# State-space layer of a decoder trunk: the convolution of x moved from channels on partitions to tokens on partitions

## The chip, the cores and the metric

The kernel runs on one core of one Trainium2 chip. The metric is device time in microseconds, the median of several executions. A core has five engines with queues of their own: PE (TensorE: matmuls; the loads of its stationary operand are shown apart as PEld), DVE (VectorE), ACT (ScalarE), POOL (GpSimd) and SP (SyncE), which only issues DMAs here. ACT and POOL issue some DMAs too.

## The reference, cut to what matters

The trunk is one latent-attention (MLA) layer and one state-space (SSM, Mamba-2) layer over 256 tokens, each followed by a dense squared-ReLU MLP; D_MODEL is 2048, the SSM's inner width 4096 (8 groups of 512 channels, 8 heads of 64 each) and everything is float32. What the change touches is this:

```python
def causal_depthwise_conv(x, w, b):            # width 4, each channel by itself
    C = x.shape[-1]
    out = lax.conv_general_dilated(
        x, w[:, None, :], window_strides=(1,), padding=[(SSM_CONV_WIDTH - 1, 0)],
        dimension_numbers=('NWC', 'WIO', 'NWC'), feature_group_count=C)
    return out + b

def ssm_mixer(h, w_in, conv_w, conv_b, ...):
    zxbcdt = h @ w_in
    z, xbc, dt = jnp.split(zxbcdt, [SSM_D_INNER, SSM_D_INNER + SSM_CONV_DIM], axis=-1)
    xbc = jax.nn.silu(causal_depthwise_conv(xbc, conv_w, conv_b))
    xs, b_in, c_in = jnp.split(xbc, [...], axis=-1)
    ...
    y = ssd_chunked_scan(xs, dt, a, b_in, c_in)    # one chunk of 256 tokens here
    y = y + d_skip * xs
    y = y * jax.nn.silu(z); y = group_rms_norm(y) * norm_g
    return y @ w_out
```

For each token and channel of x, B and C the projection is summed with the three tokens before it, by four weights, a bias is added, and silu is applied.

## The kernel before

Every matmul with a large weight goes over blocks of 512 output columns and both halves of 128 tokens (t = 0, 1). A weight is read in units of 128 x 1024 float32 (512 KB) by SP into one of six `raw` buffers (L87). ACT makes its rounded part `wh` (L102), DVE the rest `wl` (L103), four buffers of each, and PE runs 8 matmuls with wh (L325, L326) and 4 with wl (L329). `Flow.next` loads six units ahead and converts three ahead of the unit that PE is at. A block of the SSM is four pieces of two units, and after each piece `tick()` runs what was put off with `later(n, fn)`: fn runs n + 1 ticks on. The order on PE is the written one. The order on the other engines is arranged when the program is built, by when operands are expected to be ready; the written order breaks ties.

The SSM stage runs B0, dt, B1, C0, C1 and then the list `SSM_ORDER`: x blocks (projection of one group of 512 x channels), z blocks (the gate) and o blocks (output projection).

- `conv` (L1063) takes a block of x, B or C that lies with tokens on partitions (`ev`, evacuated by L1093). In each of two halves it turns 2 x 128 channels onto partitions with four PE transposes (L1070), multiplies by the last weight and adds the bias on ACT (L1076), adds the other three shifted products on DVE (L1079: weight a scalar per partition, shift along the free axis), and makes silu from tanh (L1081, L1082).
- B and C are used in that layout (`cb_group`, L1153). x is needed with tokens on partitions, so `x_block`'s `back` (L1173) turns it back, four transposes for each t (L1179), and evacuates it (L1181) into `xtm`.
- Then the eight heads of the group are put on the list `hq`; `pump`, run once a tick, takes one or two: SP reads a row of `cumD` (running sums of the decay, kept in DRAM) to all partitions (`cm`, L1215), ACT and DVE make the decayed score matrix `mt` (L1219 to L1222), and after eight heads `products` runs the matmuls with x (L1237), and POOL and DVE add the skip term (L1240 to L1243). `across` (L1193) adds the part of the first 128 tokens to the second.
- `z_block` (L1250) computes the gate; its `gate`, two ticks later, multiplies on POOL (L1268), norms, and transposes the result for the o blocks (L310).

In the two MLPs, POOL issues 56 DMAs that add a weight quarter to a buffer on arrival (L199).

Of the kernel before, what the change touches and what calls it, by code (L numbers as in the profile page):

```python
# [28 lines left out]
P = 128  # L29
# [185 lines left out]
class Trunk:  # L215
# [822 lines left out]
    def ssm_body(self, sp, dp, gain):  # L1038
# [21 lines left out]

        self.later(0, setup)

        def conv(ev, ct, dst, lag, after):  # L1063

            def half(j):
                b = self.bank(early[0])
                for k in range(2):
                    for t in range(2):
                        o = k * 256 + t * P
                        nc.tensor.transpose(b[:, o:o + P], ev[t][:, (2 * j + k) * P:(2 * j + k + 1) * P], self.ident)  # L1070
                a = self.scratch()
                for k in range(2):
                    c = ct + 2 * j + k
                    wc = lambda i: cst[:, C_CW + 4 * c + i:C_CW + 4 * c + i + 1]
                    s, o = b[:, k * 256:(k + 1) * 256], a[:, k * 256:(k + 1) * 256]
                    nc.scalar.activation(o, s, AF.Identity, bias=cst[:, C_CB + c:C_CB + c + 1], scale=wc(3))  # L1076
                    for i in (2, 1, 0):
                        m = 3 - i
                        nc.vector.scalar_tensor_tensor(o[:, m:256], s[:, 0:256 - m], wc(i), o[:, m:256], ALU.mult, ALU.add)  # L1079
                th = self.scratch()  # L1080
                nc.scalar.activation(th, a, AF.Tanh, scale=0.5)  # L1081
                nc.vector.scalar_tensor_tensor(dst(j), th, 1.0, a, ALU.add, ALU.mult)  # L1082
            self.later(lag, lambda: half(0))
            self.later(lag + 1, lambda: half(1))
            if after:
                self.later(4, lambda: after(0))
                self.later(5, lambda: after(1))

        def evac(accs):
            ev = []  # L1090
# [6 lines left out]
        def bc_block(name, i):  # L1097
            accs = self.block([("si", name, i, q) for q in range(4)], xT)
            t = self.ktile(self.k4, F32)
            fm[name, i] = t  # L1100
            conv(evac(accs), (32 if name == "B" else 40) + 4 * i,
                 lambda j: t[:, 2 * j:2 * j + 2].rearrange("p a b -> p (a b)"), 0, None)

        def dt_block():
            self.narrow_block(("si", "dt", 0, 0), self.xT, dt_chain)
# [1 line left out]
        def dt_chain(b):  # L1107
            pairs = [sp.tile([P, S], F32, tag="cm", name=f"dt{i}", bufs=4).rearrange("p (i t h) -> p i t h", i=2, t=2) for i in range(3)]
            v, e, s, z, q, la = (pairs[i // 2][:, i % 2] for i in range(6))
            for t in range(2):  # L1110
                nc.vector.scalar_tensor_tensor(v[:, t], b[:, t * 64:(t + 1) * 64], rs[t], cst[:, C_DTB:C_DTB + 64],
                                               ALU.mult, ALU.add)
            nc.scalar.activation(e, v, AF.Abs)
            nc.scalar.activation(e, e, AF.Exp, scale=-1.0)
            nc.vector.tensor_scalar(s, e, 2.0, None, ALU.add)
            nc.vector.reciprocal(s, s)
            nc.vector.tensor_tensor(s, s, e, ALU.mult)
            nc.vector.tensor_tensor(z, s, s, ALU.mult)
            nc.vector.tensor_scalar(q, z, 1.0 / 17, None, ALU.mult)
            for c in (15, 13, 11, 9, 7, 5, 3):  # L1120
                nc.vector.scalar_tensor_tensor(q, q, 1.0 / c, z, ALU.add, ALU.mult)
            nc.vector.scalar_tensor_tensor(q, q, 1.0, s, ALU.add, ALU.mult)
            nc.vector.tensor_scalar(v, v, 0.0, None, ALU.max)
            nc.vector.scalar_tensor_tensor(dt, q, 2.0, v, ALU.mult, ALU.add)
            for t in range(2):
                nc.vector.scalar_tensor_tensor(la[:, t], dt[:, t], -1.0, aneg, ALU.mult, ALU.mult)
            cum = sp.tile([64, S], F32, name="cum")

            def cums():
                b = self.bank(False)  # L1130
                nc.tensor.matmul(b[:64, 0:256], la[:, 0], tri, start=True, stop=False)
                nc.tensor.matmul(b[:64, P:256], la[:, 1], tri[:, 0:P], start=False, stop=True)
                nc.scalar.activation(cum, b[:64, 0:256], AF.Copy)
                nc.scalar.dma_start(cumD, cum)
                self.later(0, back)

            def back():
                b = self.bank(False)
                for t in range(2):
                    nc.tensor.transpose(b[:, t * 64:(t + 1) * 64], cum[:, t * P:(t + 1) * P], self.ident[:64, :64])  # L1140
                nc.tensor.matmul(b[:, 128:192], tri[:, P:256], la[:, 0], start=True, stop=True)
                nc.vector.tensor_copy(pcum.rearrange("p t h -> p (t h)"), b[:, 0:128])

                for t in range(2):
                    nc.vector.tensor_tensor(edge[:, t], b[:, 128:192], pcum[:, t], ALU.subtract)
                nc.scalar.activation(edge[:, 0], edge[:, 0], AF.Exp)
                nc.scalar.activation(edge[:, 1], edge[:, 1], AF.Exp, scale=-1.0)
                nc.vector.tensor_tensor(edge[:, 0], edge[:, 0], dt[:, 0], ALU.mult)
                nc.vector.tensor_scalar(edge[:, 1], edge[:, 1], 2.0, None, ALU.mult)

            self.later(2, cums)

        def cb_group(g):  # L1153
# [1 line left out]
            b = self.bank(early[0])  # L1155
            nc.tensor.matmul(b[:, 0:256], B[:, 0:P], C, start=True, stop=True)
            nc.tensor.matmul(b[:, 256:384], B[:, P:256], C[:, P:256], start=True, stop=True)
            t = sp.tile([P, 384], F32, name=f"cb{g}")
            for o in (0, 256):
                nc.vector.scalar_tensor_tensor(t[:, o:o + P], b[:, o:o + P], 0.125, tri[:, 0:P], ALU.mult, ALU.mult)  # L1160
            nc.scalar.activation(t[:, P:256], b[:, P:256], AF.Copy, scale=0.125)
            cb[g] = t

        def x_block(g):
            accs = self.block([("si", "x", g, q) for q in range(4)], xT)
            ev = evac(accs)
            fmx = [None, None]

            def dst(j):
                fmx[j] = self.scratch()  # L1170
                return fmx[j]

            def back(t):  # L1173
                if t == 0:
                    xg[g] = []
                b = self.bank(False)
                for k in range(4):
                    o = (k % 2) * 256 + t * P
                    nc.tensor.transpose(b[:, k * P:(k + 1) * P], fmx[k // 2][:, o:o + P], self.ident)  # L1179
                x = sp.tile([P, 512], F32, tag="xtm", name=f"xtm{g}_{t}", bufs=6)  # L1180
                nc.scalar.activation(x, b, AF.Copy)  # L1181
                xg[g].append(x)
                if t == 0:
                    return
# [6 lines left out]
                nc.gpsimd.tensor_tensor(heads_of(xw), heads_of(xg[g][0]), spread(edge[:, 0]), ALU.mult)  # L1191

                def across():  # L1193
                    b = self.bank(False)
# [16 lines left out]
        def head(g, i, dg):  # L1211
# [1 line left out]
            h = 8 * g + i  # L1213
            cm = sp.tile([P, S], F32, tag="cm", name=f"cm{h}", bufs=4)
            nc.sync.dma_start(cm, cumD[h:h + 1].to_broadcast([P, S]))  # L1215
            m = sp.tile([P, 256], F32, tag="mt", name=f"mt{h}", bufs=11)
            half = lambda t: m[:, t * P:(t + 1) * P]
            for t in range(2):
                nc.scalar.activation(half(t), cm[:, t * P:(t + 1) * P], AF.Relu, bias=pcum[:, t, h:h + 1], scale=-1.0)  # L1219
# [61 lines left out]
            assert 2 * i in gated and 2 * i + 1 in gated  # L1281
            return self.block([("so", 2 * i + q, nb) for q in range(2)], self.from_tiles(yT[2 * i:2 * i + 2]))

        bc_block("B", 0)
        dt_block()
        bc_block("B", 1)
        bc_block("C", 0)
        bc_block("C", 1)
        for g in range(GROUPS):
            self.later(2 + g % 2 + 4 * (g // 2), lambda g=g: cb_group(g))  # L1290
        self.pump = pump
        for step in SSM_ORDER:
            kind, i = step[0], int(step[1])
            if step == "x2":
                early[0] = False
            if kind == "x":
                x_block(i)
            elif kind == "z":
                z_block(i)
# [3 lines left out]
            else:  # L1303
# [81 lines left out]
def sequence(d):  # L1385
# [40 lines left out]
    si("B", 0)  # L1426
    add(("si", "dt", 0, 0), d["sidt"], 16, 64)
    si("B", 1), si("C", 0), si("C", 1)
    so = lambda k, nb: add(("so", k, nb), d["so"][k, nb])
    for step in SSM_ORDER:  # L1430
        kind, i = step[0], int(step[1])
        if kind in "xz":
            si(kind, i)
        elif i < 3:
# [85 lines left out]
```

## Time and profile before

| | |
|---|---|
| median of 3 runs | 2308.83 us (2308.43 to 2308.88) |
| span of the profiled execution | 2306.1 us; its own time is not given apart from the span |
| SSM stage in it | 952 to 1619 us |
| granted PE clock | 1.000 |
| busy: PE, DVE, ACT, POOL | 2298.4, 1890.2, 1419.4, 187.9 us |
| DMA | 510.77 MB, mean 221 GB/s |

The span runs from the first to the last instruction. Matmuls are pipelined, so a busy PE is not a PE at its peak; the cost of a PE instruction is read from the starts of its neighbours. In rows of groups the two numbers after the bar are busy time in us and mean ns of one, then idle time of the engine before them and what ended it.

### The profile page before, as it was taken

To read this page: it belongs to the slowest core of one execution; us is meant where nothing else is said; L and a number is where in the kernel's file an instruction comes from. 1 tells how busy PE (TensorE), PEld (TensorE's weight loads), DVE (VectorE), ACT (ScalarE), POOL (GpSimd) and SP (SyncE) were. 2 spreads that over 40 slices of the span, in tenths; PEclk is the share of its full clock that TensorE was granted. 3 is DMA by queue.
4 is the path that set the end of the run, shared out by engine and by line. 5 is a ranking of instruction groups with operands and counts; after the bars stand their busy time and mean duration, and the time that the engine had idled before them with its cause. 6 is when DMAs were issued, how large, how long until landed. Compare 5 with 4: busy or idle time off the path is not lost.

```text
span 2306.1 us, 30756 instructions
## 1 busy us (share of the span) xinstructions
PE 2298.4 (100%) x11057; PEld 1911.1 (83%) x11057; DVE 1890.2 (82%) x2318; ACT 1419.4 (62%) x1995; POOL 187.9 (8%) x227
## 2 busy tenths in 40 slices
PE   9999999999999999999999999999999999999999
PEld 7888888888888888888888888888888888888887
DVE  7786697999899897678788767756989989989895
ACT  7775466566666656575577555545666656666663
POOL 1430000000000000000022001110000000000000
PEclk9999999999999999999999999999999999999999
DMA  8444677877887877665566656556687788787874
GB/s 316 148 129 155 200 233 245 262 239 250 265 243 247 267 217 241 198 211 180 169 204 207 223 181 204 186 191 201 201 257 234 250 265 250 241 268 240 250 230 161
DMA packets 152153, 510.77 MB, mean 221 GB/s; under 512 B 17152, under 2 KB 26304, under 8 KB 152000
## 3 DMA queue, kind: packets, MB, share of 16 engines
q1 hardware_dynamic: 143712, 479.37, 62.7%
q0 software_dynamic: 8064, 29.36, 7.6%
q8 instruction: 87, 1.43, 0.3%
q14 instruction: 66, 0.54, 0.1%
q10 hardware_dynamic: 224, 0.07, 0.0%
HBM read 506.58 MB, written 2.16 MB: 221 GB/s over the span
## 4 chain that ended last, share of the span: by engine, by line
PE 98%; DMA 1%; DVE 0%; ACT 0%; issue 0%; SPq 0%; POOL 0%; DVEq 0%; ACTq 0%
PE acc L325 13%; PE acc L326 13%; PE acc L329 13%; PE yp L595 9%; PE yp L596 9%; PE yp L594 9%; PE st L595 8%; PE st L596 8%; PE st L594 8%; PE sm L310 2%; PE y L1237 1%; PE acc L596 1%; PE acc L595 1%; PE acc L594 1%; PE acc L703 0%; DMA wraw<-mi 0%
## 5 line engine op out<-in xcount | busy, mean ns | idle before, releaser
L102 ACT ACTIVATE wh<-wraw 128x1024 fp32r<-128x1024 f32 (+1 forms) x818 | 860.0, 1054 | 627.6 <-PE acc L326 311.0
L103 DVE TENSOR_TENSOR wl<-wraw,wh 128x1024 fp32r<-128x1024 f32 (+1 forms) x818 | 987.9, 1220 | 265.1 <-ACT wh L102 255.0
L594 PE MATMUL yp<-wh,k 128*128 128x512 f32 x896 | 349.8, 390 | 0.0
L595 PE MATMUL yp<-wl,k 128*128 128x512 f32 x896 | 348.9, 389 | 0.5 <-DVE wl L103 0.4
L596 PE MATMUL yp<-wh,k 128*128 128x512 f32 x896 | 348.8, 389 | 0.0
L325 PE MATMUL acc<-wh,xt 128*128 128x512 f32 x704 | 280.8, 399 | 1.3 <-ACT wh L102 1.3
L326 PE MATMUL acc<-wh,xt 128*128 128x512 f32 x704 | 274.6, 390 | 0.0
L102 ACT ACTIVATE wh<-wrx 128x1024 fp32r<-128x1024 f32 x168 | 177.9, 1059 | 136.3 <-PE yp L596 108.0
L103 DVE TENSOR_TENSOR wl<-wrx,wh 128x1024 fp32r<-128x1024 f32 x168 | 204.0, 1219 | 38.5 <-ACT wh L102 38.3
L595 PEld LDWEIGHTS yp<-wl,k 128*128 128x128 f32 x896 | 168.2, 188 | 36.0 <-DVE wl L103 1.4
L596 PEld LDWEIGHTS yp<-wh,k 128*128 128x128 f32 x896 | 168.2, 188 | 35.0
L594 PEld LDWEIGHTS yp<-wh,k 128*128 128x128 f32 x896 | 168.2, 188 | 34.6
L325 PE MATMUL acc<-wh,k 128*128 128x512 f32 x496 | 196.7, 397 | 0.0
L326 PE MATMUL acc<-wh,k 128*128 128x512 f32 x496 | 193.3, 390 | 0.0
L329 PE MATMUL acc<-wl,xt 128*128 128x512 f32 x704 | 188.4, 389 | 0.0
L594 PE MATMUL st<-wh,xt 128*128 128x512 f32 x448 | 176.8, 395 | 0.0
L595 PE MATMUL st<-wl,xt 128*128 128x512 f32 x448 | 174.8, 390 | 0.0
L596 PE MATMUL st<-wh,xt 128*128 128x512 f32 x448 | 174.8, 390 | 0.0
L325 PEld LDWEIGHTS acc<-wh,xt 128*128 128x128 f32 x704 | 132.3, 188 | 29.7 <-ACT wh L102 2.8
L329 PEld LDWEIGHTS acc<-wl,xt 128*128 128x128 f32 x704 | 132.1, 188 | 27.9
L326 PEld LDWEIGHTS acc<-wh,xt 128*128 128x128 f32 x704 | 132.3, 188 | 26.9 <-issue 1.0
L199 POOL DMA_DIRECT2D wrx<-mi x56 | 48.8, 872 | 1140.3 <-DVE wl L103 1034.3
(302 smaller groups left out, 3458.8 us busy)
## 6 DMA issues: line engine op xcount, KB each, us to landing
wraw<-mi SPq DMA_DIRECT2D x256, 512.0 KB, 5.2
wraw<-mo SPq DMA_DIRECT2D x256, 512.0 KB, 5.3
wraw<-si SPq DMA_DIRECT2D x160, 512.0 KB, 4.5
wraw<-so SPq DMA_DIRECT2D x64, 512.0 KB, 4.3
wrx<-mi SPq DMA_DIRECT2D x56, 512.0 KB, 5.0
wrx<-mi POOLq DMA_DIRECT2D x56, 512.0 KB, 8.1
wraw<-wo SPq DMA_DIRECT2D x32, 512.0 KB, 3.8
wraw<-ukv SPq DMA_DIRECT2D x16, 512.0 KB, 4.1
```

The costliest lines, as they stand in the source:

```text
L102: self.last = nc.scalar.activation(h[:, v], raw[:, v], AF.Copy)
L103: nc.vector.tensor_tensor(lo[:, v], raw[:, v], h[:, v].bitcast(F32), ALU.subtract)
L199: nc.gpsimd.dma_start(st["b11"].tile, quarter(d, 1, 0), accum_op=ALU.add)
L310: self.nc.tensor.transpose(b[:, j * P:(j + 1) * P], src[:, j * P:(j + 1) * P], self.ident)
L325: nc.tensor.matmul(accs[t][:, :n], ah, wh[:, q, :], start=first and kt + q == 0, stop=False)
L326: nc.tensor.matmul(accs[t][:, :n], al, wh[:, q, :], start=False, stop=False)
L329: nc.tensor.matmul(accs[t][:, :n], lhs(kt + q, t)[0], wl[:, q, :], start=False, stop=en and q == nk - 1)
L594: nc.tensor.matmul(b, ah, wh, start=first and q == 0, stop=False)
L595: nc.tensor.matmul(b, ah, wl, start=False, stop=False)
L596: nc.tensor.matmul(b, al, wh, start=False, stop=last and q == 1)
L1237: nc.tensor.matmul(y[t][c, o], part(t)[:, c], xg[g][t][:, o], start=True, stop=True)
```

## The change

x is convolved where it lies, with tokens on partitions, so that a shift by a token is a shift of partitions. The evacuated block goes into `xt` (2 x 512 columns) and is written by an ACT-issued DMA to a DRAM scratch `xD` that has three rows of zeros in front. Two ticks later SP reads, for each t, the three earlier tokens of every row in one DMA into `taps` (128 partitions, 3 x 512). DVE multiplies them by weights that are repeated on all partitions (`cw`, read for each x block, one buffer), and adds the four products and the bias. No x block uses PE for it. The steps are spread over the eight ticks after the block; the old chain ended six ticks after it. B and C keep `conv`. B1 and C1 move between the first x blocks, dt behind B0. To make room, mt goes from 11 to 9 buffers, cb from 8 tiles to 5 rotating ones, cum into a scratch tile, and the descriptor scratch of POOL's DMAs is set to 2048.

```diff
+        taps = sp.tile([P, 2, 3, 512], F32, name="taps")
+        xD = dp.tile([S + 3, GROUPS * 512], F32, name="xD")
+
+        def zeros():
+            z = self.scratch()[:96, :P]
+            nc.gpsimd.memset(z, 0.0)
+            nc.gpsimd.dma_start(xD[0:3].rearrange("r (q n) -> (r q) n", n=P), z)
+
+        self.later(1, zeros)
...
-            cum = sp.tile([64, S], F32, name="cum")
+            cum = self.scratch()[:64, :S]
...
-            t = sp.tile([P, 384], F32, name=f"cb{g}")
+            t = sp.tile([P, 384], F32, tag="cb", name=f"cb{g}", bufs=5)
...
         def x_block(g):
+            cw = []
+
+            def weights():
+                cw.append(sp.tile([P, 2560], F32, tag="cw", name=f"cw{g}", bufs=1))
+                nc.sync.dma_start(cw[0], d["cwx"][g])
+
+            self.later(2, weights)
             accs = self.block([("si", "x", g, q) for q in range(4)], xT)
-            ev = evac(accs)
...
-            def back(t):
...
-                for k in range(4):
-                    o = (k % 2) * 256 + t * P
-                    nc.tensor.transpose(b[:, k * P:(k + 1) * P], fmx[k // 2][:, o:o + P], self.ident)
-                x = sp.tile([P, 512], F32, tag="xtm", name=f"xtm{g}_{t}", bufs=6)
-                nc.scalar.activation(x, b, AF.Copy)
...
+            xt = sp.tile([P, 2, 512], F32, tag="xtm", name=f"xtm{g}", bufs=3)
+            x = [xt[:, t] for t in range(2)]
+            th = [None, None]
+            for t in range(2):
+                nc.scalar.activation(x[t], accs[t], AF.Copy, scale=rs[t])
+            nc.scalar.dma_start(xD[3:S + 3, g * 512:g * 512 + 512].rearrange("(t p) n -> p t n", t=2), xt)
+
+            def shift():
+                for t in range(2):
+                    v = xD[t * P:t * P + P, g * 512:g * 512 + 512]
+                    row = v.ap[0][0]
+                    nc.sync.dma_start(taps[:, t], bass.AP(tensor=v.tensor, offset=v.offset, ap=[[row, P], [row, 3], [1, 512]]))
+
+            def mult(t):
+                flat = taps[:, t].rearrange("p i n -> p (i n)")
+                nc.vector.tensor_tensor(flat, flat, cw[0][:, :1536], ALU.mult)
+                nc.vector.tensor_tensor(x[t], x[t], cw[0][:, 1536:2048], ALU.mult)
+
+            def total(t):
+                for v in (taps[:, t, 2], taps[:, t, 1], taps[:, t, 0], cw[0][:, 2048:]):
+                    nc.vector.tensor_tensor(x[t], x[t], v, ALU.add)
+                th[t] = self.scratch()
+                nc.scalar.activation(th[t], x[t], AF.Tanh, scale=0.5)
+
+            def silu(t):
+                nc.vector.scalar_tensor_tensor(x[t], th[t], 1.0, x[t], ALU.add, ALU.mult)
+
+            def ahead():
+                xg[g] = x
...
-            conv(ev, 4 * g, dst, 0, back)
+            self.later(1, shift)
+            if g >= 4:
+                self.later(0, lambda: cb_group(g))
+            self.later(3, lambda: mult(0))
+            self.later(4, lambda: total(0))
+            self.later(5, lambda: mult(1))
+            self.later(6, lambda: (silu(0), total(1)))
+            self.later(7, lambda: (silu(1), ahead()))
...
-            m = sp.tile([P, 256], F32, tag="mt", name=f"mt{h}", bufs=11)
+            m = sp.tile([P, 256], F32, tag="mt", name=f"mt{h}", bufs=9)
...
-        bc_block("B", 0)
-        dt_block()
-        bc_block("B", 1)
-        bc_block("C", 0)
-        bc_block("C", 1)
-        for g in range(GROUPS):
-            self.later(2 + g % 2 + 4 * (g // 2), lambda g=g: cb_group(g))
-        self.pump = pump
         for step in SSM_ORDER:
             kind, i = step[0], int(step[1])
-            if step == "x2":
+            if step == "C1":
                 early[0] = False
-            if kind == "x":
+            if kind in "BC":
+                bc_block(kind, i)
+                if step == "C0":
+                    for g in range(4):
+                        self.later(2 + g % 2 + 4 * (g // 2), lambda g=g: cb_group(g))
+                    self.pump = pump
+            elif kind == "d":
+                dt_block()
+            elif kind == "x":
...
-SSM_ORDER = ["x0", "x1", "x2", "z0", "x3", "z1", "x4", "z2", "o0", "x5", "z3", "x6", "z4", "o1",
+SSM_ORDER = ["B0", "d0", "C0", "x0", "B1", "x1", "C1", "x2", "z0", "x3", "z1", "x4", "z2", "o0", "x5", "z3", "x6", "z4", "o1",
              "x7", "z5", "z6", "o2a", "z7", "o2b", "o3"]
...
+    taps = np.concatenate([f(ssm_conv_w)[0], f(ssm_conv_b)], 0)[:, :4096]
+    a["cwx"] = rows(taps.reshape(5, 8, 512).transpose(1, 0, 2), 2560)
...
-    nc = bacc.Bacc("TRN2", target_bir_lowering=False, num_devices=1)
+    nc = bacc.Bacc("TRN2", target_bir_lowering=False, num_devices=1, dynamic_dma_scratch_size=2048)
```

More of the change, by code (lines that the diff above doesn't have):

```diff
@@ L1061, in ssm_body, with conv @@
         self.later(0, setup)
-        def conv(ev, ct, dst, lag, after):
+        taps = sp.tile([P, 2, 3, 512], F32, name="taps")
[5 more added lines that the diff above has]
+        self.later(1, zeros)
+        def conv(ev, ct, dst, lag):
             def half(j):
@@ L1084, in conv @@
             self.later(lag + 1, lambda: half(1))
-            if after:
-                self.later(4, lambda: after(0))
-                self.later(5, lambda: after(1))
         def evac(accs):
@@ L1101, in bc_block @@
             conv(evac(accs), (32 if name == "B" else 40) + 4 * i,
-                 lambda j: t[:, 2 * j:2 * j + 2].rearrange("p a b -> p (a b)"), 0, None)
+                 lambda j: t[:, 2 * j:2 * j + 2].rearrange("p a b -> p (a b)"), 0)
         def dt_block():
@@ L1190, in back @@
                 xw = self.scratch()
-                nc.gpsimd.tensor_tensor(heads_of(xw), heads_of(xg[g][0]), spread(edge[:, 0]), ALU.mult)
+                nc.gpsimd.tensor_tensor(heads_of(xw), heads_of(x[0]), spread(edge[:, 0]), ALU.mult)
                 def across():
@@ L1425, in sequence @@
     si = lambda name, i: [add(("si", name, i, q), d["si"][q, col(name, i)]) for q in range(4)]
-    si("B", 0)
-    add(("si", "dt", 0, 0), d["sidt"], 16, 64)
-    si("B", 1), si("C", 0), si("C", 1)
     so = lambda k, nb: add(("so", k, nb), d["so"][k, nb])
@@ L1431, in sequence @@
         kind, i = step[0], int(step[1])
-        if kind in "xz":
+        if kind in "xzBC":
             si(kind, i)
+        elif kind == "d":
+            add(("si", "dt", 0, 0), d["sidt"], 16, 64)
         elif i < 3:
```

10 lines of the change are left out of this document (removed).

## The prediction

> **What bounds the kernel now.** I read the page first, then the stages, then the rows of the SSM stage. The page and the stages (each row: window, length, then busy time and count of PE, weight loads, DVE, ACT, POOL, then clock, DMA share, GB/s):
>
> ```profile
> span 2306.1 us, 30756 instructions
> PE 2298.4 (100%) x11057; PEld 1911.1 (83%) x11057; DVE 1890.2 (82%) x2318; ACT 1419.4 (62%) x1995; POOL 187.9 (8%) x227
> PE 98%; DMA 1%; DVE 0%; ACT 0%; issue 0%; SPq 0%; POOL 0%; DVEq 0%; ACTq 0%
> ...
> 10.00:20.00 10.00, 9.15 (x40) 7.23 (x40) 8.53 (x16) 9.21 (x17) 0.00 (x0) 1.00 1.03 411
> 600.00:644.00 44.00, 44.00 (x200) 36.44 (x199) 38.56 (x40) 29.87 (x33) 0.87 (x1) 1.00 0.85 272
> 952.00:1619.00 667.00, 666.81 (x3507) 550.96 (x3506) 488.90 (x694) 391.99 (x622) 77.17 (x59) 1.00 0.62 196
> 1149.00:1281.00 132.00, 132.00 (x812) 108.81 (x809) 114.19 (x173) 93.31 (x183) 32.81 (x24) 1.00 0.66 207
> ```
>
> The chain is 98% PE, and in the SSM stage (952 to 1619) PE is idle 0.2 us of 667, at clock 1.00. So every microsecond that leaves PE's stream there leaves the time, until another engine gets late. The next is DVE: 489 of 667 us over the stage, 114 of 132 (87%) in its densest part. DMA moves 196 GB/s there; the same engines have moved 411.
>
> The span is 2306.1; the profiled execution's own time is not given beside it, and the median of the runs is 2308.83, so 2.7 us lie around the span. I take what the span loses off the median.
>
> **PE: what goes.** PE's timeline, start and length, around a tick with two batches of transposes:
>
> ```profile
> 1098.02 1.07 PE L329 MATMUL acc<-wl,xt 128*128 128x512 f32 x4
> 1100.74 1.07 PE L329 MATMUL acc<-wl,xt 128*128 128x512 f32 x4
> 1101.65 0.60 PE L1179 MATMUL sm<-cst,s 128*128 128x128 f32 x4
> 1102.09 0.60 PE L1070 MATMUL sm<-cst,s 128*128 128x128 f32 x4
> ...
> 1104.37 1.08 PE L329 MATMUL acc<-wl,xt 128*128 128x512 f32 x4
> ```
>
> One weight unit (8 matmuls with wh, 4 with wl) recurs every 1100.74 - 1098.02 = 2.72 us; with two batches of four transposes between, after 3.63. A batch costs (3.63 - 2.72)/2 = 0.455 us, although its matmuls read 0.60: the pipelining hides the rest. An x block has two batches forward (L1070) and two back (L1179); eight blocks make 32 batches: 32 x 0.455 = 14.6 us. The forward ones of B and C stay. Nothing is added to PE; cb groups, B1 and C1 only change places. Bounds of this term: 14.6, to 15.0 if a batch is taken at 0.47.
>
> **DVE: what comes.** Rows of groups (busy, mean ns) and of source lines (min/median/max):
>
> ```profile
> L103 DVE TENSOR_TENSOR wl<-wraw,wh 128x1024 fp32r<-128x1024 f32 x205 | 255.5, 1248 | 128.9 <-ACT wh L102 127.5
> L396 DVE TENSOR_TENSOR s<-x,gb 128x512 f32<-128x512 f32 x24 | 15.4, 684 | 0.0
> L518 DVE TENSOR_TENSOR xf<-xf,xf 128x1024 f32<-128x1024 f32 x8 | 9.7, 1217 | 0.0
> L1222 DVE SCALAR_TENSOR_TENSOR mt<-mt,dt,cb 128x128 f32<-128x128 f32 x128 | 52.7, 463 | 1.6 <-ACT mt L1220 1.4
> ...
> L1079 DVE SCALAR_TENSOR_TENSOR s<-sm,cst,s x114: 469/480/484, 979.4 to 1481.5; 128x255 f32<-128x255 f32 x38, 128x254 f32<-128x254 f32 x38, 128x253 f32<-128x253 f32 x38
> L1082 DVE SCALAR_TENSOR_TENSOR s<-s,s x16: 678/684/1534, 1085.1 to 1483.2; 128x512 f32<-128x512 f32 x16
> L1222 DVE SCALAR_TENSOR_TENSOR mt<-mt,dt,cb x128: 332/346/1458, 1067.9 to 1455.0; 128x128 f32<-128x128 f32 x128
> L1240 POOL TENSOR_TENSOR xtm<-xtm,gb 128x512 f32<-128x512 f32 x16 | 20.6, 1310 | 154.2 <-PE y L1237 115.2 <-issue 38.8
> ```
>
> Old x block: 12 x 0.480 (L1079) + 2 x 0.684 (L1082) = 7.1 us. New, per token half: one product of 1536 columns, one of 512, four sums of 512, one last step like L1082. 512 columns take 0.684 and 1024 take 1.217, so 512 more cost 0.533 and 1536 take 1.75. A half is 1.75 + 5 x 0.684 + 0.684 = 5.85, a block 11.7: 4.6 us more, 37 us over eight. None of it is on PE's path while DVE's lateness stays under the cover. The cover: wh and wl have four buffers, so a unit's weights may be refilled three units (8.16 us) ahead, wl is first needed 8/12 into its unit (1.81), and the two conversions take 1.06 and 1.25 (L102, L103): 8.16 + 1.81 - 2.31 = 7.7 us.
>
> I added up DVE's work tick by tick (a tick is two units) in the new order, and carried over what did not fit into PE's time. The worst block is x2, because C1's old-style convolution now lands in the same ticks as x1's new chain: 8 conversions 9.9 + C1's 7.1 + x1's two sums, second product and last steps 9.3 + three heads 2.5 + two steps after the head products 1.4 = 30.2 us, against PE's 8 x 2.72 + C1's two batches 0.9 + one y group 2.0 = 24.7. It runs 5.5 late, on top of nearly 1 from before: 6.5, under 7.7. After x3, x4 and in o0 the lateness peaks at 4 to 6.5 and drains each time. The same sum for the old order gives 504 us over the stage where the row above measures 489, so it errs high. By it PE waits for nothing, with a margin of about 1 us.
>
> What eats the margin: the old steps read PSUM, and L1079 never took more than 484 ns; ops whose operands both lie in SBUF (L1222) have a median of 346, a mean of 463 and a maximum of 1458, about one POOL operation (1.31) longer. The change puts 96 such ops in place of 96 of the PSUM kind. At the loss of L103 (1.248 against the 1.217 of L518, 0.03 each) they cost 3 us more in all, at L1222's 0.12 each 11 us. I take 5, nearer to the large ops, which the new ones resemble, and half of it at the peaks where it reaches PE: 2.4 us. [...] If every new op that meets POOL were held for a whole POOL operation, this term would grow; that is a rival below.
>
> **ACT.** Out go four L1076 and two L1181 per block, in comes one more DMA issue. ACT is at 392 of 667, so this is worth nothing; loads of ACT only fall.
>
> **DMA and SP.** Landing times and SP's own waits:
>
> ```profile
> wraw<-si SPq DMA_DIRECT2D x160, 512.0 KB, 4.5
> cumD<-cum ACTq DMA_DIRECT2D x1, 64.0 KB, 4.3
> gb<-dsk SPq DMA_DIRECT2D x8, 256.0 KB, 2.8
> ...
> SPq L87 <- DVE wl L103: 424.8, 190, 3.9
> SPq L1215 <- DMA cumD<-cum: 4.1, 1, 4.1
> ...
> L102 ACT ACTIVATE wh<-wraw 128x1024 fp32r<-128x1024 f32 x205 | 216.8, 1059 | 214.8 <-PE acc L326 199.1 <-issue 10.0 <-DVE xtm L1243 3.9
> L1093 ACT ACTIVATE s<-acc,rs 128x512 f32<-128x512 f32 x24 | 15.0, 674 | 0.0
> ```
>
> Each x block adds 1.31 MB of weights (cw), 0.52 MB written to xD and 1.57 MB of taps read back: 27 MB, on 131 MB (196 GB/s x 667 us). 158 MB over 652 us is 242 GB/s, less than the 272 of the MLP row, where PE also never waits. The rate is covered; order is what matters. The store: 2 x 0.67 for the two evacuations, 4.3 to land as cumD's (64 KB), 1.1 to 1.5 more for 450 KB at 411 or 314 GB/s (207/0.66): xD is there some 7 us after the block's end. The taps take 2.1 of latency (2.8 less 0.6 of transfer) and 3.8 to 5.0 of transfer: by 14 us. The first product stands four ticks (21.8 us) after the block's end, so it waits for nothing.
>
> Queued behind them on SP are weight loads and cm loads. SP is mostly idle, waiting for raw buffers to come free (425 us, 190 times); six raw buffers turn over in 6 x 2.72 = 16.3 us, of which 4.5 + 2.3 are used, so a load may be 9.5 us late before wh starts late, and some 7 more before PE sees it. One shift: up to 4.1 of waiting for the store, as cumD's, and 3.8 to 5.0 of taps in front: 9, inside 16.
>
> **Smaller edits.** The chain around three products, and the rows of the heads on ACT:
>
> ```profile
> 1148.38 2.02 PE y L1237 x64
> 1180.61 2.02 PE y L1237 x64
> 1217.33 2.02 PE y L1237 x64
> ...
> L1219 ACT ACTIVATE mt<-cm,pcum 128x128 f32<-128x128 f32 x128 | 45.1, 391 | 12.0 <-DMA cm<-cumD 9.3 <-PE y L1237 1.6 <-DVE s L1079 1.2
> L1220 ACT ACTIVATE mt<-mt 128x256 f32<-128x256 f32 x64 | 26.0, 406 | 0.3
> ```
>
> mt from 11 to 9 buffers holds one batch of eight and one ahead; the products (y) come 32 to 37 us apart and eight heads need 8 x (2 x 0.391 + 0.406) = 9.5 on ACT: nothing, or one head's wait. xtm is now taken at the block's end instead of five ticks later, and x3 needs z0's gate two ticks before: it needs what POOL and DVE do in that time, and the other acc pair covers 21.8 us. Rotating cb buffers were last read three groups before: nothing. The x chain ends two ticks later; o3 alone follows, with z7's gate two ticks after z7 in o2b and o2b's and o3's first blocks as cover. The smaller descriptor scratch touches the POOL loads of the MLPs (next part).
>
> **Sum.** 2308.8 - 14.6 + 2.4 = 2296.6 us.
>
> **Rivals.**
>
> 1. DVE becomes the bound (0.19). For it: the 6.5 of 7.7 above, and the op that meets POOL. POOL is busy 33 of 132 us in the dense part: if a quarter of 96 ops waits half a POOL operation, 96 x 0.25 x 0.65 = 16 us, of which half falls on blocks without room. PE then waits 6 to 10 us: 2300 to 2304, so 2302. Against it: L103's mean has risen by only 0.03. [...]
>
> 2. The other side: SP's queue (0.23). cw has one buffer, so the weights of x(g+1) wait on SP for DVE's last sum of x(g), which stands in the same tick wherever two x blocks are eight ticks apart: x1, x2, x3, x4, x6. If DVE is 6 late there, SP stands 6 + 3.4, then 1.31 MB pass (3.2 to 4.2), and three ticks later the taps bring 9 more before the queue has recovered: 19 to 23 us against 16. It decides from 16.6 us on. Price: about 5 us at each of five places, 25 in all: 2319. A lighter case, 2 us at each, gives 2304 to 2306. Against it: SP issues ahead of need almost always, and a backlog drains at (314 - 207) GB/s.
>
> 3. The POOL loads of the MLPs get slower with the smaller scratch (0.04):
>
> ```profile
> wrx<-mi POOLq DMA_DIRECT2D x56, 512.0 KB, 8.1
> ...
> POOL wrx L199 <- DVE wl L103: 1034.3, 54, 39.6
> ```
>
> They land in 8.1 us, and the written order of the MLP lets a sum be used 12 us after its first half. Past 12, half a microsecond at each of 56 is 28: 2322. Against: POOL idles 1034 us ahead of these 56, so few are in flight at once.
>
> 4. It doesn't do what it says: the transposes were hidden anyway (0.04). Then 2309 to 2311. Against: the 0.91 us between the starts above.
>
> **How the numbers follow.** The forecast has 0.50, with its own range 2293.5 (no wait at all, and 15.0 off) to 2300. Rivals 0.19, 0.23, 0.04, 0.04. A measurement of this kernel can tell about 0.2%, 4.6 us, from no change: 2304.2 to 2313.4 is "same". Faster: 0.50 + 0.18 of rival 1 = 0.68. Same: 0.01 of rival 1, 0.06 of rival 2, 0.03 of rival 4: 0.10. Slower: 0.17 of rival 2, 0.04 of rival 3, 0.01: 0.22. Range 2293 to 2314 holds the forecast, rival 1, rival 4 and the lighter half of rival 2; rivals 2 and 3 in full, about 0.2, stay out.
>
> **What would show it.** Right: no L1179 and a third of the L1070 rows on PE; the SSM stage about 652 us long; DVE near 525 us in it, over 95% in x1 to z2; PE idle under 3 us there, released by wl; POOL loads in the MLPs at 8 us still. Wrong: PE idle of more than 6 us with DVE wl as releaser (rival 1); PE or ACT waiting for wraw or cm DMAs, and SP waiting for xD or for DVE's sums (rival 2); an MLP stage that is longer than before (rival 3).

## The result, and the profile after

The change makes the kernel slower: 2317.11 us (median of 5 runs, 2315.75 to 2320.61) against 2308.43 (5 runs, 2307.7 to 2308.88), a ratio of 1.0042 [1.0030, 1.0054]: 0.4% slower, clear of the interval. The profiled execution of the changed kernel took 2318.87 us, with a span of 2317.1.

The page after, its head, its chain, and the landing times of the new transfers (the last three rows are from the view of DMA issues):

```profile
span 2317.1 us, 30468 instructions
PE 2291.6 (99%) x10929; PEld 1898.5 (82%) x10929; DVE 1922.5 (83%) x2318; ACT 1387.8 (60%) x1947; POOL 198.5 (9%) x229
PE 36%; DMA 1%; DVE 1%; issue 0%; ACT 0%; POOL 0%; SPq 0%; DVEq 0%; POOLq 0%
...
taps<-xD SPq DMA_DIRECT2D x16, 768.0 KB, 7.4
cw<-cwx SPq DMA_DIRECT2D x8, 1280.0 KB, 8.1
xD<-xtm ACTq DMA_DIRECT2D x8, 512.0 KB, 6.6
```

PE is 6.8 us less busy than before (2298.4), and the span is 11.0 longer: work has left PE, and more than that has come back as idle time. All of it lies in the SSM stage. From the first MLP's start to its last matmul it is 631 us in both traces, and the second MLP takes 675 to 676 in both.

The SSM stage by windows (columns as in the prediction) and the waits of PE, DVE and SP in it (engine, instruction, what it waited for: us in all, times, longest):

```profile
952.00:1630.00 678.00, 659.21 (x3378) 537.40 (x3377) 521.46 (x694) 360.30 (x574) 88.16 (x59) 1.00 0.73 231
```

```profile
PE acc L329 <- DVE wl L103: 13.3, 14, 2.0
PE acc L325 <- ACT wh L102: 5.4, 3, 2.2
...
DVE xtm L1196 <- DMA xD<-xtm: 27.6, 8, 4.8
DVE taps L1195 <- DMA taps<-xD: 19.9, 8, 4.2
...
SPq L1191 <- DMA xD<-xtm: 41.5, 8, 6.3
SPq L1176 <- DVE xtm L1200: 8.3, 7, 2.4
```

PE was idle 0.2 us in this stage before; now it is idle 18.8, and 13.3 of that ends when DVE delivers a `wl`. DVE in turn stands 47.5 us, in 16 waits, in front of two of its new instructions: L1196, the product of x with its own weight, and L1195, the product of the taps. L1196 waits for the store: it multiplies x in place, and the store still reads x. L1195 waits for the taps to land.

DVE's timeline shows what stands behind these waits. x3's block ends at 1180.0 us, when ACT begins its evacuation (start, length, instruction, idle time before it):

```profile
1182.86 1.23 DVE L103 TENSOR_TENSOR wl<-wraw,wh 128x1024 fp32r<-128x1024 f32 x1 [1.50 <-ACT wh L102]
1187.68 0.69 DVE L1196 TENSOR_TENSOR xtm<-xtm,cw 128x512 f32<-128x512 f32 x1 [3.59 <-DMA xD<-xtm]
1188.29 1.22 DVE L103 TENSOR_TENSOR wl<-wraw,wh 128x1024 fp32r<-128x1024 f32 x1
...
1194.40 1.76 DVE L1195 TENSOR_TENSOR taps<-taps,cw 128x1536 f32<-128x1536 f32 x1 [2.37 <-DMA taps<-xD]
1196.07 1.22 DVE L103 TENSOR_TENSOR wl<-wraw,wh 128x1024 fp32r<-128x1024 f32 x1
```

The first product starts 7.7 us after the block's end and the taps' product 14.4 after it; in the written order both stand in the fourth tick, at 21.8. A conversion follows each at once: it could have run during the wait (its `wh` was ready at 1184.4 and 1187.0), but it stands behind the product in DVE's order. PE feels both: it waits 0.86 us for the first of these conversions, at 1189.56, and 2.04 for the second (PE's timeline, same columns):

```profile
1197.35 1.76 PE L329 MATMUL acc<-wl,xt 128*128 128x512 f32 x4 [2.04 <-DVE wl L103]
1198.91 0.63 PE L325 MATMUL acc<-wh,xt 128*128 128x512 f32 x1
1199.33 0.63 PE L326 MATMUL acc<-wh,xt 128*128 128x512 f32 x1
```

The matmuls after it start 0.42 us apart, where 0.23 is usual, until 1201.04. More often the lateness shows later, when the gate of z brings DVE its next full ticks: ten of the 17 waits, 11.5 us of the 18.7, end 34 to 42 us after an x block's end. The two longest of them, 2.01 and 2.24 us for `wh`, end at 1215.74 and 1269.99, some 21 us after a taps' product (1194.40, 1248.65). No instruction waits there for a DMA of x. Ahead of the first, ACT, which makes `wh`, had stood 5.4 us for DVE's sums and 4.4 for POOL's gate, so part of the lateness reaches PE by way of ACT.

The sum nearly closes. By how much the starts of consecutive matmuls of weight units exceed 0.2275 us, added up over the SSM stage, is 8.4 before and 32.5 after: 24.1 lost, of which 18.7 is idle time that the waits show and the rest slower and sparser matmuls behind them. 24.1 - 14.6 = 9.5, against the 11.0 by which the two spans differ; 1.5 is left over.

### The profile page after: what moved, and what is told of

The parts are those of the page before. It is cut to its first block, busy times and chain, and to the rows that moved or that the text cites. A ratio compares the mean times of both kernels' runs of the same rounds, so it can differ in the third digit from the quotient of the medians.

```text
span 2317.1 us, 30468 instructions
## 1 busy us (share of the span) xinstructions
PE 2291.6 (99%) x10929; PEld 1898.5 (82%) x10929; DVE 1922.5 (83%) x2318; ACT 1387.8 (60%) x1947; POOL 198.5 (9%) x229
## 5 line engine op out<-in xcount | busy, mean ns | idle before, releaser
L329 PE MATMUL acc<-wl,xt 128*128 128x512 f32 x704 | 190.4, 392 | 10.1 <-DVE wl L103 10.0
```

What stands on the lines that cost most here:

```text
L329: nc.tensor.matmul(accs[t][:, :n], lhs(kt + q, t)[0], wl[:, q, :], start=False, stop=en and q == nk - 1)
```

## The experiments

Three theories stand against each other. W: DVE's waits for the store and the taps, at the places where those instructions stand in DVE's order. D: DVE's larger work alone. B: the DMA side, the bytes or SP's queue. All diffs are against the changed kernel, unless it is said otherwise, and every ratio is against the kernel before.

**Neither wait (e3).** The taps are read from the weights, which are in DRAM from the start, with as many bytes, and x's product goes to a scratch instead of in place. No tap holds x.

```diff
-  nc.sync.dma_start(taps[:, t], bass.AP(... xD ...))
+  nc.sync.dma_start(taps[:, t].rearrange("p i n -> p (i n)"), d["cwx"][g][:, :1536])
-  nc.vector.tensor_tensor(x[t], x[t], cw[0][:, 1536:2048], ALU.mult)
+  p[t] = self.scratch()
+  nc.vector.tensor_tensor(p[t], x[t], cw[0][:, 1536:2048], ALU.mult)   # sums and silu then on p[t]
```

> Leaves out the shift: the taps are read from the weights' tensor in DRAM (same 768 KB each, no wait for the store to xD), and the product of x goes to a scratch tile, so that it does not wait for the store either. The store, the bytes and all DVE work stay. W: nearly all of the loss comes back, 2294 to 2301. D: DVE has the same work, 2312 to 2320. B: 2312 to 2320.

Measured: 2293.01 us (2292.31 to 2293.18), ratio 0.9931 [0.9916, 0.9946], 15.8 us faster than before, just under what W gave. The stage of this kernel (the window ends where the second MLP starts, some 8 us further on than the windows above), and the taps' product in it (count, length in ns as min/median/max, first and last start in us):

```profile
952.00:1612.00 660.00, 660.00 (x3421) 545.38 (x3420) 515.27 (x701) 369.90 (x583) 78.78 (x59) 1.00 0.72 237
...
L1193 DVE TENSOR_TENSOR taps<-taps,cw x16: 1741/1754/2153, 914.6 to 1414.5; 128x1536 f32<-128x1536 f32 x16
```

PE is busy all 660 us, and the run has the transfers of the change in number and size and its DVE instructions in number and shape. But they do not stand where they stood. Taps that need no store are read early, and their product follows them: in the eight blocks the first one starts between 112 us before the block's end and 6.7 after it, where the change has it 12.8 to 17.2 after. Of the 16 products, 28 us of work, eight run before the block's end, six of them 38 us or more before it. So e3 takes the waits away and moves DVE's work as well. It shows that PE's saving is there to be had; it doesn't tell W from D, and it reads the taps' bytes at other times, so it doesn't settle B either. e10 and e12 below do, with all of the work behind the block. DVE still stands 15.9 us in this run, for `cw`, and PE doesn't feel it; there is room for some waiting.

**Less work, same waits (e4).** Three of the four sums of each half are left out, 48 instructions of 0.684 us.

```diff
-  for v in (taps[:, t, 2], taps[:, t, 1], taps[:, t, 0], cw[0][:, 2048:]):
+  for v in (taps[:, t, 2],):
```

> Leaves out three of the four sums in each half of an x block (the convolution is incomplete): 8 x 6 x 0.684 = 33 us less DVE work, nearly the 37 that the change added. All DMAs and waits stay. D: the loss goes, 2294 to 2300. W: the waits at the products stay, only the stalls that come later in the block shrink: 2306 to 2313. B: 2314 to 2320.

Measured: 2297.32 us (2296.15 to 2298.58), ratio 0.9950 [0.9935, 0.9965]. DVE's and PE's waits in this kernel:

```profile
DVE xtm L1196 <- DMA xD<-xtm: 21.8, 7, 4.4
DVE taps L1195 <- DMA taps<-xD: 20.5, 8, 3.9
...
PE acc L329 <- DVE wl L103: 3.6, 5, 1.0
```

This is the time that D gave, and W's, 2306 to 2313, did not come. But DVE stands 42.3 us, nearly as long as with the change, and PE loses only 3.6. So the waits cost only together with the work: 33 us less of it makes room for nearly all of them.

**One wait of the two (e6).** The taps come from the weights as in e3, but the product of x stays in place and waits for the store (diff: the first half of e3's).

> Leaves out the shift: taps are read from the weights' tensor, so that neither SP nor the taps wait for the store; the product of x stays in place, so that DVE still waits for the store. If DVE's wait for the store carries the loss: 2308 to 2314. If SP's wait and the late taps carry it: 2292 to 2297.

Measured: 2299.24 us (2296.48 to 2300.78), ratio 0.9961 [0.9947, 0.9975]. DVE stands 24.2 us for the store. The time lies between the two expectations. From e3 the wait for the store costs 7 us (15.8 faster than before, then 8.8). The taps' products run early here too, 6 to 111 us before the block's end, so the 17.5 from here to the change (8.7 slower) is not the price of the wait for the taps alone: the products also move behind the block, and SP again stands for the store.

**The wait for the store taken away (e5).** x's product goes to a scratch (the second half of e3's diff), and the taps are those of x.

> The product of x goes to a scratch tile (as in the run without waits), so that DVE no longer waits for the store that still reads x; taps come from xD as in the changed kernel. If DVE's wait for the store (28 us in the changed kernel) carries the loss: 2302 to 2309. If SP's wait for the store, with late weight loads behind it, carries it: 2313 to 2320. If it takes both, in between, 2308 to 2314.

Measured: 2325.87 us (2325.32 to 2326.98), ratio 1.0077 [1.0062, 1.0092], slower than the change and than all three expectations. The wait moved:

```profile
DVE taps L1195 <- DMA taps<-xD: 41.6, 8, 7.3
DVE s L1197 <- DMA cw<-cwx: 5.4, 2, 2.7
...
PE acc L325 <- ACT wh L102: 11.7, 4, 3.5
PE acc L329 <- DVE wl L103: 10.2, 11, 2.5
```

DVE stands 47.0 us, as before in two parts and now mostly in one, of up to 7.3 us at a time. Taking away what makes one instruction wait is worth nothing while the next one in order needs the same store first.

**The taps issued by POOL (e2).**

```diff
-  nc.sync.dma_start(taps[:, t], ...)
+  nc.gpsimd.dma_start(taps[:, t], ...)
```

> The taps' DMAs are issued by POOL instead of SP, so that SP no longer stands in front of the store to xD. W: weight and cm loads are no longer late (ACT waits for them 21 and 36 us in the changed kernel), DVE's own waits stay: 2304 to 2313. D: nothing changes, 2314 to 2320. B: same bytes on the same engines, 2314 to 2320.

Measured: 2331.71 us (2330.72 to 2333.31), ratio 1.0100 [1.0085, 1.0115], slower than any of the theories gave. SP no longer waits for the store; POOL does, and the taps land later (9.6 us from issue instead of 7.4):

```profile
taps<-xD POOLq DMA_DIRECT2D x16, 768.0 KB, 9.6
...
DVE taps L1195 <- DMA taps<-xD: 34.2, 13, 6.3
DVE xtm L1196 <- DMA xD<-xtm: 26.9, 8, 4.1
```

DVE's waits grow by 13.6 us (47.5 to 61.1) and the time by 14.2 (22.9 over before instead of 8.7).

**SP's wait taken away (e7).** e5, with the shift a tick later and behind that tick's weight load on SP.

```diff
-  self.later(1, shift)
+  self.later(2, shift)
+  with self.tc.issue_after(self.flow.last_ld.ins):   # around the taps' dma_start
```

> Product of x out of place, and the taps' issue moved one tick later in the written order and queued on SP behind the weight load of that tick, two loads further back than before: SP should find the store landed. If SP's head-of-line wait carries the loss: 2296 to 2304. If the lateness of the taps on DVE carries it, they are later still: 2312 to 2322.

Measured: 2319.32 us (2316.63 to 2320.92), ratio 1.0047 [1.0032, 1.0062]. SP stands 10.1 us at the store instead of 35.4 in e5, and the kernel is 6.5 us faster than e5 and still slow; DVE stands 32.1 us for the taps and 4.2 for `cw`. So SP's queue is at most a part of it; e10 and e12 below show that SP may stand nearly as long as with the change in a fast kernel.

**The products held at their written place (e1).** Each pair of products is put behind the `wl` conversion of its own tick.

```diff
+  with self.tc.issue_after(self.flow.last_lo.ins):   # around both products in mult
```

> Theory W (waits): in the changed kernel DVE starts the products of an x block long before the tick in which they are written and stands there until the store to xD (28 us in all) and the taps (20 us) have landed, with the weight conversions behind it; SP stands at the taps' issue (42 us) with the weight loads behind it. This kernel queues each product on DVE behind the conversion of its own tick, and changes nothing else. W: DVE's 48 us of waits go, SP's stay, and 7 to 15 us come back: 2302 to 2310. Theory D (DVE has too much work): the work is the same and later, so no gain: 2314 to 2320. Theory B (DMA traffic): same bytes, 2314 to 2320.

Measured: 2326.66 us (2321.23 to 2328.51), ratio 1.0075 [1.0058, 1.0091]. None of the theories gave this. The waits for the DMAs are gone, and PE hardly waits for `wl` any more, but:

```profile
PE sm L310 <- DVE s L1306: 18.2, 10, 6.3
PE acc L325 <- ACT wh L102: 2.2, 2, 1.4
PE acc L329 <- DVE wl L103: 1.9, 2, 1.6
```

L310 are the transposes of the gated z, which PE reaches at a place fixed in its order. By the trace, the products in the fourth and sixth tick push the sums behind them, then the gate, and PE stands up to 6.3 us at a time. The granted clock of the stage was 0.98.

**The taps' product held in the third tick (e8, e10, e11).** e8 is e7 with the taps' product behind the conversion of the third tick after the block. e10 is e5 with that hold alone, so the taps are issued as in the change. e11 is e8 with the tanh on ACT held behind its tick's conversion.

```diff
+  self.later(2, lambda: held.append(self.flow.last_lo))      # e10; e8 and e11 note it in shift
+  with self.tc.issue_after(held[0].ins):                     # around the taps' product in mult
+  with self.tc.issue_after(self.flow.last.ins):              # e11, around the tanh in total
```

> As the one before, and the products of the taps queued on DVE behind the conversion of the tick in which the taps are issued (some 16 us after the block's end by the old order's rows, five less than in the kernel that holds all products to their tick). If DVE standing in front of the taps carries what is left: 2294 to 2301. If a later x chain makes the gates of the z blocks late, as when all products were held: 2312 to 2326.

> Product of x out of place and the products of the taps queued on DVE behind the conversion of the third tick, but the taps' issue left on SP where the change has it, so that SP still waits for the store (42 us there). If DVE standing in front of the taps carried the loss and SP's wait nothing: 2299 to 2306, like the kernel that also moved the issue. If SP's wait costs by itself: 2308 to 2316.

> The fastest correct kernel so far, and the tanh queued on ACT behind the conversion of the tick in which it is written, so that ACT does not stand in front of DVE's sums (66 us there) with the conversions of wh behind it. If ACT's standing costs PE time: 2295 to 2301. If ACT has room for it: 2301 to 2305. If the later tanh makes the gates of the z blocks late: 2306 to 2315.

Measured: e8 2302.98 us (2301.55 to 2306.22), 0.9979 [0.9970, 0.9988]; e10 2298.44 (2295.45 to 2300.8), 0.9955 [0.9940, 0.9970]; e11 2302.77 (2301.78 to 2306.26), 0.9978 [0.9968, 0.9987]. Waits of e10:

```profile
DVE taps L1196 <- DMA taps<-xD: 4.6, 3, 1.7
DVE s L1198 <- DMA cw<-cwx: 3.3, 2, 2.5
...
PE acc L325 <- ACT wh L102: 1.4, 4, 0.6
PE sm L1163 <- DVE k L300: 0.8, 1, 0.8
...
SPq L1191 <- DMA xD<-xtm: 37.0, 8, 7.1
```

e8 lies between its two expectations, e10 just under its first. e10's edit differs from e5's in the hold of 16 instructions alone, and is 28 us faster, though the first taps' product of each block starts at nearly the same time in both (12.8 to 16.5 us after the block's end in e5, 13.3 to 16.5 in e10). Of the kernels with the whole computation it has the lowest median, 10.0 us under the kernel before. SP stands at the store as long as in e5 (37.0 against 35.4 us), and PE loses 2.2. Moving the taps' issue later (e8) only brings DVE's wait for them back (10.8). The hold of the tanh (e11) changes nothing: ACT stands 65.6 us for DVE's sums in both.

**The change with nothing but the hold (e12).** Both products, in place as they were, are held behind the conversion of the third tick.

```diff
+  held = []
+  self.later(2, lambda: held.append(self.flow.last_lo))
+  with self.tc.issue_after(held[0].ins):                     # around both products in mult
```

> The changed kernel with one thing altered: all products of an x block (in place, as in the change) are queued on DVE behind the conversion of the third tick after the block. DVE's waits for the store and for the taps should be nearly gone, SP's stay. If the place of the products on DVE is the whole cause: 2296 to 2302, as with the product out of place. If the in-place product costs by itself: 2304 to 2312. If any hold of the x product makes the chain late, as the hold to the fourth and sixth tick did: 2315 to 2327.

Measured: 2300.46 us (2299.97 to 2302.54), ratio 0.9968 [0.9956, 0.9980]; from 8.7 us slower than before to 7.8 faster. Of the waits for DMAs of x one is left, and PE waits at the gates alone:

```profile
DVE taps L1196 <- DMA taps<-xD: 2.5, 1, 2.5
...
SPq L1191 <- DMA xD<-xtm: 38.4, 8, 6.4
...
PE sm L310 <- DVE s L1308: 5.5, 4, 2.1
```

The same block x3, which ends at 1171.27 us in this kernel, on DVE:

```profile
1186.23 1.76 DVE L1196 TENSOR_TENSOR taps<-taps,cw 128x1536 f32<-128x1536 f32 x1 [2.54 <-DMA taps<-xD]
1187.91 1.22 DVE L103 TENSOR_TENSOR wl<-wraw,wh 128x1024 fp32r<-128x1024 f32 x1
1189.04 0.69 DVE L1197 TENSOR_TENSOR xtm<-xtm,cw 128x512 f32<-128x512 f32 x1
```

The taps' product now comes first, 12.9 to 16.5 us after the block's end in the eight blocks, and x's product 2.8 us or more behind it. In the changed kernel x's product starts after 6.6 to 10.4 us, its wait included, and the taps' product after 12.8 to 17.2, about as here. What the hold takes away is the standing, since DVE does its conversions in that time. Of PE's waits for `wl` and `wh` none is left. In e1 the first taps' product starts after 18.6 to 24.1.

e10 and e12 decide between the theories. Both do the whole work of the change behind the block and move its bytes, with SP standing nearly as long (37.0 and 38.4 us, 41.5 in the change), and both are faster than before: D and B in their plain form fall. What is left is W, as a matter of the place in DVE's order; that there is so little room for a wait comes from the work, as e4 shows.

**The side edits alone (e9).** The kernel before with the new order of B1, C1 and dt, mt 9, cb 5, the cum scratch and the descriptor scratch, but its old convolution of x.

> The kernel before with all of the change but the convolution: new order of B1, C1 and dt, nine mt buffers, rotating cb, cum in a scratch tile, the small descriptor scratch; x still by transposes. If these side edits cost nothing, as forecast: 2307 to 2311. If the order or the buffers carry the loss: 2315 or more.

Measured: 2310.93 us (2310.23 to 2312.79), ratio 1.0011 [1.0001, 1.0020]: 0.2 to 4.6 us slower, below what the prediction called a difference. PE waits 2.2 us in it, once, for the old convolution.

Put together, with DVE's standing for the DMAs of the convolution (store, taps, `cw`) in the stage:

| kernel | DVE stands, us | against before, us |
|---|---|---|
| e3 neither wait, taps' products early | 17.1 | -15.8 |
| e4 both waits, 33 us less work | 42.3 | -11.5 |
| e10 out of place, third tick | 7.9 | -10.0 |
| e6 store's wait only, taps' products early | 32.8 | -8.8 |
| e12 in place, third tick | 2.5 | -7.8 |
| e11 as e8, tanh held | 15.2 | -5.6 |
| e8 as e10, taps issued later | 15.7 | -5.1 |
| the change | 47.5 | +8.7 |
| e7 out of place, taps issued later | 36.3 | +11.3 |
| e5 out of place | 47.0 | +17.8 |
| e1 fourth and sixth tick | 0 | +17.9 |
| e2 taps issued by POOL | 61.1 | +22.9 |

The sum of waiting does not rank them: e1 stands nowhere and is among the slowest. By the traces, what counts is whether a conversion, or the work of a gate, comes late behind the products.

## Why the prediction was wrong, point by point

**PE's term was right.** It took off 14.6 us, with 15.0 as the bound. e3, in which PE waits for nothing, is 15.8 faster than before (12 to 19 by its interval).

**DVE's durations were right but for one.** The new instructions in the SSM stage of the changed kernel (busy, mean ns of one, idle before):

```profile
L1200 DVE TENSOR_TENSOR xtm<-xtm,taps 128x512 f32<-128x512 f32 x48 | 31.7, 684 | 0.0
L1195 DVE TENSOR_TENSOR taps<-taps,cw 128x1536 f32<-128x1536 f32 x16 | 28.1, 1755 | 19.9 <-DMA taps<-xD 19.9
L1205 DVE SCALAR_TENSOR_TENSOR xtm<-s,xtm 128x512 f32<-128x512 f32 x16 | 16.3, 1021 | 0.0
...
L1196 DVE TENSOR_TENSOR xtm<-xtm,cw 128x512 f32<-128x512 f32 x16 | 10.9, 688 | 27.6 <-DMA xD<-xtm 27.6
```

1.75 and 0.684 were forecast. The last step, L1205, took 1.021 in the mean instead of 0.684: 5.4 us over 16. A block is then 3.5 + 1.4 + 5.5 + 2.0 = 12.4 us instead of 11.7.

**The term for contention was right in its sum on DVE, by luck, and wrong in its places.** It spread 5 us over the 96 new instructions with two SBUF inputs and put 2.4 of it on PE. In the changed kernel all of the loss, 5.4 us, lies on L1205, which was not among the 96. Its six slow instructions, of 1.40 to 1.77 us, are those that ran beside POOL's product of the gate; the 64 sums, with a maximum of 695 ns, met nothing on POOL but products of two columns. In e12 it is the sums that meet it:

```profile
L1201 DVE TENSOR_TENSOR xtm<-xtm,taps x48: 675/683/1785, 1048.4 to 1491.6; 128x512 f32<-128x512 f32 x48
```

Six of these took 1.78, each beside POOL's product of the gate; two sums that met POOL's skip product kept 0.68, and there POOL's instruction took 3.7 us instead of some 1.3. The old step L1089, with one input in SBUF and one in PSUM, ran beside POOL six times in the changed kernel and took 0.48 as always. In the kernel before, L1079 had met POOL once, for 0.12 us, so its even times showed nothing yet. What the 5.4 us cost PE isn't known: four of the slow L1205 start 3 to 4 us before the end of a wait of PE (the one at 1212.15, for one), but in e12 PE waits for no `wl` or `wh`. For the same reason the lateness by work alone, forecast at 6.5 of a cover of 7.7, fits e12; e3 doesn't test it.

**The failed step is the sentence "The first product stands four ticks (21.8 us) after the block's end, so it waits for nothing."** The transfers were sized well enough: the store lands 6.6 us after its issue, where 5.4 to 5.8 was put, and the taps 7.4 after theirs, where 5.9 to 7.1 was put. But a product's place in DVE's order is not its written tick. The order is arranged when the program is built, by when operands are expected to be ready, and it put the product of x 7.7 us after the block's end and the taps' product at 14.4. Over the eight blocks it is 6.6 to 10.4 and 12.8 to 17.2, waits included. Both came ahead of conversions and before their data. The front part of this document says how the order is made; the prediction counted written ticks all the same. Then the same 7.7 us of cover that the work had nearly used had to pay for a wait of 2.5 to 4.8 us and a second of 1.4 to 4.2, in every x block. e12's edit holds nothing but the two products and gives 2300.5 instead of 2317.1; e10 against e5 shows the same for the taps' product alone, 28 us. These two show the step as the cause.

**DMA and SP were nearly right.** The rate, 242 GB/s forecast, is 237 where PE doesn't wait (e3). SP stands 5.2 us for each store, where up to 4.1 was put; in e10 and e12 it stands 4.6 and 4.8, and they are faster than before.

**The smaller edits were put at nothing** and measured at 0.2 to 4.6 us.

**The rivals.** The second gave 2319, the nearest number, for another reason: SP's wait for `cw` to come free is 8.3 us in all, and not 6 + 3.4 at each of five places. Its signs came too: SP waited for xD, and ACT waited 24.5 us for weights and 35.5 for `cm` (none and 9.3 before). They are not the cause, for in e10 SP waits 37.0 for xD and ACT 15.6 and 24.7, and e10 is fast. The first named the sign that appeared, PE idle for more than 6 us with `wl` as the releaser (13.3), and the reason that DVE is late; but it made it late by contention with POOL, and so came to 2302. The third is out: the adding loads of POOL land in 8.2 us (8.1 before), and the MLPs are as long as they were. The fourth is out by e3. Missing was a rival in which DVE stands, in its order, for a DMA, with conversions behind it.

**What stays open.** Why e5 is 9 us slower than the change, with the same 47 us of standing on DVE, is read from the trace alone: the waits are longer one by one (7.3 against 4.8) and ACT stands 60.0 us at the tanh instead of 27.3, so that `wh` comes late too (11.7 us on PE). The granted clock also falls behind three of PE's waits in e5 (0.64 over 1236 to 1239, 0.50 over 1292 to 1296 and over 1442 to 1445), and behind one in the change (0.77 over 1195 to 1200). None of this was tried apart; e11's hold on ACT, in a kernel without that loss, changed nothing. The 8.0 us between e12 and e3 are likewise not split beyond the 5.5 that PE waits at the gates; e3 has half of the taps' products ahead of their blocks, which e12 can't have.

## What to carry to other kernels

Where a program's order is arranged by expected readiness, an instruction that is fed by a DMA stands where the arranger thinks that the data lands; read its real place from the timeline of a like instruction, and ask what is queued behind it on its engine. If that engine has little room and feeds the bound, pin the instruction behind the last urgent piece of work that fits before the landing: here the arranged place cost some 17 us and the written one some 26 against one in between. To price such a wait, feeding the same instruction with data that is there from the start is not enough: the arranger then moves the instruction as well, here by up to 112 us ahead of the block, and the kernel shows what the change is worth without the wait and with that work elsewhere. Hold the instruction at one place in the order, with the wait and without it.

## What the runs showed of the hardware that was not expected

**The clock gave way after short pauses of PE, and not after each.** Three windows of 5 us of the changed kernel:

```profile
1195.00:1200.00 5.00, 2.96 (x9) 2.13 (x8) 5.00 (x5) 2.03 (x3) 0.00 (x0) 0.77 0.99 376
1265.00:1270.00 5.00, 2.76 (x13) 1.82 (x12) 4.65 (x4) 3.16 (x7) 4.20 (x4) 1.00 0.91 321
1270.00:1275.00 5.00, 4.40 (x50) 3.23 (x52) 4.39 (x7) 4.45 (x7) 0.54 (x1) 1.00 0.52 166
```

In the first, PE stood 2.04 us and the granted clock fell to 0.77 over the window, and the matmuls started 0.42 us apart for some 2 us more; in the second it stood 2.24 and the clock stayed at 1.00, in the third too. e5 repeats it: after a pause of 2.57 us that ended at 1180.32 the clock was 1.00 over 1180.5 to 1183.5, after one of 2.47 that ended at 1235.85 it was 0.64 over 1236 to 1239. Why one of two nearly equal pauses was followed by a lower clock and the other was not, no run shows.

**A round trip through DRAM took 14 us here:** 6.6 for the store of 512 KB and 7.4 for 768 KB of taps, with DMA at 231 GB/s over the stage; issued by POOL the taps took 9.6.
